# Value products of an attention group: two runs of five key tiles in place of four of two or three

## Chip, cores and metric

The kernel runs on one core of a Trainium2 chip. The metric is the device time in microseconds (us) from launch to end; three runs of the kernel before were timed. TensorE (PE in the rows; PEld is its loading of weights), VectorE (DVE), ScalarE (ACT) and GpSimd (POOL) each issue their instructions in one fixed order, and semaphores tie them together.

## What is computed

A trunk of two layers over 1024 latent and 256 context tokens. Each layer has an input projection, three head groups (latent attention, a convolution module, an mLSTM), an output projection with a norm, and an MLP with a norm. The change is in the latent attention. Cut to that part, the reference is:

```
def attend(q, k, v):
    s = einsum('bhqd,bhkd->bhqk', q, k) * 96 ** -0.5
    p = softmax(s, axis=-1)
    return einsum('bhqk,bhkd->bhqd', p, v)     # 8 heads, q and k of 96, v of 64 columns
```

There are 8 heads. Latent queries (1024) see 1280 keys, which are ten key tiles of 128; in the first layer the 256 context queries see the two key tiles of the context.

## The kernel before

`attention` (line 792) works on **groups** and **units**. A group is a pair of heads and 256 queries. A unit is one head and 128 queries, so a latent group has four units; they are called here the first, second, third and fourth unit of a group. The groups run over four head pairs, and within a pair over four latent blocks of 256 queries. In the first layer the fourth block of a pair has six units, since the two context units lie between its own.

For unit i the loop at line 987 issues, in this order:

- the **scores**: nine products in three chunks of keys (512, 512 and 256 columns), lines 77 to 79, tile `sc`. `sc` has 2560 columns, 1280 for the even units and 1280 for the odd ones; the two halves meet inside one bank of PSUM (columns 1024 to 1535);
- between the chunks, the **transposes** of the exponentials of unit i - 2 (line 936, ten blocks of 128 x 128 in parts of four, four and two), each part into one bank of PSUM (`et_ps`) and from there by ScalarE to the buffer `et` (line 84);
- the **softmax** (lines 908 to 911): VectorE reads the unit's scores from PSUM, negates them and takes the row minimum on the way (called the read below), ScalarE takes the exponentials and their sums, VectorE the reciprocals (`rb`);
- what `plan` holds for unit i. `at(i, ...)` appends to it. `values(G, j0, j1, fin)` (line 948) issues the value products of group G for the key tiles j0 to j1 (line 861, tile `pv`), for each tile one of either head: the two heads take the two halves of TensorE's columns. A product of f32 operands is two instructions, so a key tile is four. With `fin` it also issues `norm` (line 864): two transposes of the reciprocals on TensorE, two instructions on VectorE (lines 870 and 871), and `spill` (line 497): a copy and a subtraction on GpSimd and two stores from the SP queue. `qproj` (line 837) projects the queries of one head of the next group: six products on TensorE into a bank (`q_ps`), and its splitting on VectorE and ScalarE (`qf`, `kq`).

```
for k, (j0, j1) in enumerate(((0, 3), (3, 5), (5, 8), (8, 10))):
    at(f + 6 + k, lambda G=G, j0=j0, j1=j1: values(G, j0, j1, j1 == 10))
```

Here f is the number of the group's own first unit. A group of four units thus has its value products behind the scores of the next group's third unit (three key tiles) and fourth unit (two), and of the first unit (three) and second unit (two, and `norm`) of the group after that. The projections for the next group stand behind the second and third unit. While the convolution's taps last, one tap of it on VectorE (line 443) follows the scores of three units in four.

`et_ps`, `q_ps` and some other tiles share two banks of PSUM (pool `aux`, line 1997, `bufs=2`). A bank comes free when ScalarE or VectorE has read what is in it.

The order that each engine gets is set when the kernel is built: a planner of the framework takes instructions in the order in which the program issues them, but where by its own account of durations the next one of an engine would wait, it puts a later one that is ready ahead of it. On the chip each engine then keeps that order.

Of the kernel before, what the change touches and what calls it, by code (L numbers as in the profile page):

```python
# [33 lines left out]
# columns of the regrouped input projection: a0 g0 | a1 g1 | mq | mk | mv mg | mo | cq ckv kr  # L34
COL_CONV, COL_MQ, COL_MK, COL_MV, COL_MO, COL_CQ = 0, 512, 768, 1024, 1296, 1552

# per-partition constants of a layer
# [8 lines left out]
class Kern:  # L46
# [11 lines left out]
    # ---------------------------------------------------------------- helpers  # L58
# [4 lines left out]
    def after(self, ins, prev):  # L63
        """issue ins behind prev (same engine)"""
        self.tc.add_manual_dep(ins.ins, prev.ins.name, mybir.DependencyInfo(
            mybir.DependencyClass.NoSync, mybir.DependencyReason.DATA), reason="pace")
        return ins

    def release_held(self, prev, n=1):
        """the n oldest sets of transposes kept back are issued behind prev"""  # L70
        for _ in range(min(n, len(self.held))):
            for ins in self.held.pop(0):
                self.after(ins, prev)
# [20 lines left out]
    def rsqrt_steps(self, pool, out, x, scale, eps, n):  # L94
        """out = 1 / sqrt(x * scale + eps) on [p, n], from an integer estimate and Newton steps; an instruction a step."""
        p = out.shape[0]
# [14 lines left out]
    def rsqrt_act_steps(self, pool, out, x, scale, eps, n=1):  # L111
        """The same from ScalarE's square root and a Newton step."""
# [18 lines left out]
    # ---------------------------------------------------------------- set-up  # L131
# [28 lines left out]
    def ada_steps(self, l, rounds, raw_pool, ps, sm_pool, bufs, sm_tag="ada_bs", tag="wada", ahead=None, div=1):  # L160
        """Modulation vectors, four 512-column chunks a round: 0 sh1 sc1, 1 g1 sh2, 2 sc2 g2. A list of closures,
        each the products of one loaded piece and the load of a later one."""
# [48 lines left out]
    def ada_first(self, raw_pool, ps, sm_pool, bufs):  # L211
        """sh1 and sc1 of the first layer by halves of the features. A closure a half."""
# [3 lines left out]
        def half(h):  # L216
# [4 lines left out]
            # even k in the rows 0:64, odd k in the rows 64:128  # L221
# [20 lines left out]
    # ---------------------------------------------------------------- split streams: hi / lo tiles [128, tile, k, 128 tokens]  # L242
# [14 lines left out]
    def make_u0(self, u, tmp, kk):  # L257
        """The modulated stream of the first layer, four feature blocks."""
# [9 lines left out]
    # ---------------------------------------------------------------- input projection  # L268
    def load_w(self, pool, src, c0, n, tag="w"):
        """columns c0:c0+n of a [128, 8, N] weight as split tiles of four k each."""  # L270
# [25 lines left out]
    # ---------------------------------------------------------------- phase 1: everything read from the modulated stream  # L296
    def p1_mlstm(self, l, u, last, ps, wp, hk, ml, steps, w=None):
        """mLSTM query (feature-major), key, value and gates (token-major)."""
# [12 lines left out]
        # the first layer's stream comes by halves of its features  # L311
# [36 lines left out]
    def residual_steps(self, l, pool):  # L348
        """Closures: alpha * (normalised stream * ln2_g + ln2_b) of the layer before, a token tile each, in place."""
# [16 lines left out]
    def residual_consts(self, l, pool, tag, bufs):  # L366
        """Constant part of the second residual, alpha * ln1_b + g2 * b_mlp2, of both kinds of tokens to DRAM."""
# [10 lines left out]
    def p1_conv(self, l, u, last, ps, wp, tmp):  # L378
        """Gated linear unit of the conv group (twice its value; the halves are in the taps)."""
# [17 lines left out]
    def p1_mla(self, l, u, last, ps, wp, wx, raw):  # L397
        """Compressed q / kv and the rotary key of a token tile, with the mean squares of their rms norms."""
# [25 lines left out]
    # ---------------------------------------------------------------- conv: depthwise taps, layer norm over channels, swish  # L424
    def conv_steps(self, l, last, ps, acc, tp, pool):
        """Closures in order: taps of channel half 0 on VectorE, half 1 on GpSimd, then the norm and swish."""
# [7 lines left out]
        def tap(t, dve, pool_):  # L434
            # behind the given instructions of the two engines
# [61 lines left out]
    def spill(self, pool, c, t0, src):  # L497
        """256 tokens of a row block of the concatenated heads, split and kept in DRAM until the output projection."""
# [6 lines left out]
    # ---------------------------------------------------------------- bidirectional mLSTM  # L505
    def mlstm_gates(self, ps, gp, sm):
        """Stabilised gate quantities. Row r = dir * 64 + tile * 4 + head, tokens along the free axis."""
# [70 lines left out]
        # decay of every chunk on the partitions of its head  # L578
# [15 lines left out]
    def mlstm(self, l, last, ps, ml, wk):  # L594
        nc = self.nc
        nto = NLT if last else NT
        # chunk states: every chunk's own update goes to its successor's slot, then the recurrence runs in place
# [72 lines left out]
    def mlstm_out(self, l, u, last, pm, wp, S, wk):  # L670
        """Output gate from its own projection, per-head normalisation of a pair of token tiles; its rows of the
        concatenated heads."""
# [18 lines left out]
        def pair(t0):  # L691
# [6 lines left out]
            # statistics of the eight (tile, head) rows; H holds twice the gated value  # L698
# [12 lines left out]
    # ---------------------------------------------------------------- latent attention  # L711
    def mla_norm(self, l, last, gi, tmp):
        """Normalised compressed q / kv of a group of tokens, in place."""
# [11 lines left out]
    def mla_rotate(self, tmp):  # L725
        """Rotary shared key, in place."""
# [13 lines left out]
    def mla_prep(self, l, last, ps, A, tmp, gi):  # L740
        """Compressed q / kv and the shared key of a group of tokens, feature-major, the former split."""
# [28 lines left out]
    def mla_values(self, l, ps, wq, A):  # L770
        """Values of all heads, token-major."""
# [20 lines left out]
    def attention(self, l, last, psc, ps, X, wq, A1, A, B, wqk0, taps, post):  # L792
        """Software pipeline over units of (head, 128 queries): scores of unit i are issued between the transposes of
        unit i - 2, the value products of an earlier group and the projections of a later one. The units of the
        context queries (256 of a head in one) lie between those of the last latent group of their head pair."""
        nc, a = self.nc, self.a
        sc = psc.tile([P, 2560], F32, name="sc")
        # buffers in the place of the stream: transposed exponentials; split keys and queries
# [116 lines left out]
        def transpose_parts(i, E, kts):  # L915
# [11 lines left out]
            while i0 < nk:  # L927
                # runs of consecutive key tiles, four to a bank
# [25 lines left out]
        for G, (p, g) in enumerate(groups):  # L954
# [6 lines left out]
            if g < 3 or last:  # L961
                units += [(G, *x) for x in four]
                tap_at |= {f, f + 1, f + 2}
                for k, (j0, j1) in enumerate(((0, 3), (3, 5), (5, 8), (8, 10))):
                    at(f + 6 + k, lambda G=G, j0=j0, j1=j1: values(G, j0, j1, j1 == 10))
# [53 lines left out]
    # ---------------------------------------------------------------- rows, norms  # L1019
# [5 lines left out]
    def row_stats(self, pool, r, sm, tagp, junk, jb=2):  # L1025
        """(-mean, 1/std, -mean/std) of a token tile [128, 1024]; its row sums are in sm, else VectorE alone takes them."""
# [15 lines left out]
    def row_stats_steps(self, pool, st, r, sm, junk, jb, root=False):  # L1042
        """The same from row sums, the instructions behind the squares one by one."""
# [12 lines left out]
    def norm_rows(self, pool, r, sm, tagp, junk, jb=2):  # L1056
        """r = (r - mean) * rstd over the 1024 columns of a token tile."""
        st = self.row_stats(pool, r, sm, tagp, junk, jb)
        return self.nc.scalar.activation(r, r, AF.Identity, scale=st[:, 1:2], bias=st[:, 2:3])

    def next_stream(self, ps, x, t0, nt, rows, sc, sh, tmp, tag, hold=False):
        """rows: normalised token tiles t0..t0+nt; writes x = split(rows^T * sc + sh)."""
# [13 lines left out]
    def affine_cols(self, l, g0, b0, sc, sh, name):  # L1076
        """per-feature scale and shift of a modulated layer-normed stream: g*sc1, b*sc1 + sh  ([128, k, 2])"""
# [9 lines left out]
    # ---------------------------------------------------------------- output projection, first layer norm  # L1087
# [3 lines left out]
    def to_mats(self, ps, rows, sc, sh, pool, hold=False):  # L1091
        """rows: an even and an odd normalised token tile. For each kk the blocks B of rows^T * sc + sh (feature blocks
# [1179 lines left out]
```

## Time and profile before

| what | us |
|---|---|
| three runs of the kernel | 3289.71, 3295.98, 3297.98 |
| median of the runs | 3295.98 |
| span of the profiled execution, first to last instruction | 3292.5 |
| attention of the first layer, in the span | about 386 to 746 |
| attention of the second layer, in the span | about 2136 to 2469 |

The profiled execution shows its span and no time beside it; the span lies inside the three runs, 3.5 us under their median. In the rows a line is: start in us from the span's start, duration in us, engine, line of the kernel, operation, tile written and tiles read, shapes, how many were merged into the row (x12), and in brackets the idle time before it with what ended it. Matmuls are pipelined: one that shows 0.39 us may have its successor start 0.23 us after it, so distances between starts tell more than durations.

### The profile page before, as it was taken

The page shows a single profiled execution, that of the slowest core. Times are in us where ns is not written, and L with a number is a line of the kernel's source. Part 1 is how long each engine was busy: PE and PEld are TensorE (multiplying, and loading weights), DVE is VectorE, ACT ScalarE, POOL GpSimd, SP SyncE. Part 2 cuts the span into 40 slices and gives each one's busy share as a digit, 9 for nine tenths or more (in the row PEclk, how much of TensorE's full clock was granted, in tenths as well). Part 3 has the DMA queues.
Part 4 walks back from the last instruction along what each step waited for, and adds up shares of the span by engine and source line. Part 5 has one row for each costly group of instructions (what it writes and reads, how often), then busy time and mean ns, then how long its engine had stood idle before and what let it go on. Part 6 is the DMA issues. An engine that isn't in the chain of part 4 may idle for free.

```text
span 3292.5 us, 49295 instructions
## 1 busy us (share of the span) xinstructions
PE 3124.8 (95%) x18778; PEld 2540.8 (77%) x18778; DVE 2153.8 (65%) x3914; ACT 1356.8 (41%) x2572; POOL 1322.3 (40%) x1138
## 2 busy tenths in 40 slices
PE   7999999999899999999998999999999899999986
PEld 4778877777789999766677777877767799977775
DVE  3275688755854433767779445588757855578997
ACT  2122566672433333432332621466663433343332
POOL 0021488320221111466665251266411422258885
PEclk9999999999899999999999998999999899999998
DMA  8521100026433233444334332100025333333322
GB/s 263 187 68 40 49 18 17 14 83 225 159 120 101 97 99 103 157 126 144 114 109 134 142 111 50 56 21 14 14 92 213 109 109 108 106 128 97 102 94 105
DMA packets 179021, 337.17 MB, mean 102 GB/s; under 512 B 14016, under 2 KB 85696, under 8 KB 178784
## 3 DMA queue, kind: packets, MB, share of 16 engines
q1 hardware_dynamic: 178784, 334.03, 31.6%
q8 instruction: 147, 2.41, 0.3%
q14 instruction: 90, 0.74, 0.1%
HBM read 253.05 MB, written 80.92 MB: 101 GB/s over the span
## 4 chain that ended last, share of the span: by engine, by line
PE 71%; DVE 14%; issue 5%; POOL 3%; ACT 3%; DMA 3%; SPq 0%; DVEq 0%; POOLq 0%; ACTq 0%
PE c_ps L1365 18%; PE o_ps L1365 13%; PE pv L861 4%; PE et_ps L936 4%; PE ada L185 3%; PE cx_ps L1365 3%; DVE acc L2168 2%; PE sc L77 2%; PE sc L78 2%; PE sc L79 2%; PE o_ps L658 1%; PE y_ps L79 1%; DMA W<-md 1%; POOL h_s L2168 1%; PE y_ps L77 1%
## 5 line engine op out<-in xcount | busy, mean ns | idle before, releaser
L1365 PE MATMUL c_ps<-xs_hi,wm 128*128 128x256 f32 x2560 | 511.1, 288 | 11.5 <-DVE rw L2168 8.1
L1365 PEld LDWEIGHTS c_ps<-xs_hi,wm 128*128 128x128 f32 x2560 | 422.1, 195 | 38.7 <-DVE hb L1427 11.7
L1365 PE MATMUL o_ps<-xs_hi,xs_lo 128*128 128x512 f32 x1458 | 380.1, 398 | 27.8 <-DVE acc L2168 20.7
L1365 PE MATMUL c_ps<-xs_lo,wm 128*128 128x256 f32 x1280 | 366.6, 286 | 3.2 <-DVE xs_lo L2168 3.2
L1365 PEld LDWEIGHTS o_ps<-xs_hi,xs_lo 128*128 128x128 f32 x1458 | 271.9, 190 | 120.8 <-DVE acc L2168 34.6
L2168 DVE TENSOR_TENSOR acc<-o_ps,acc 128x512 f32<-128x512 f32 x405 | 271.8, 683 | 101.7 <-PE o_ps L1365 99.4
L1365 PEld LDWEIGHTS c_ps<-xs_lo,wm 128*128 128x128 f32 x1280 | 249.6, 195 | 3.9 <-DVE xs_lo L2168 3.6
L84 ACT COPY et<-et_ps 128x512 f32<-128x512 f32 (+1 forms) x392 | 198.4, 515 | 97.7 <-PE et_ps L936 93.1
L1365 PE MATMUL c_ps<-bx,wm 128*128 128x256 f32 x1536 | 229.2, 288 | 4.5 <-ACT bx L2168 3.0
L92 DVE TENSOR_TENSOR wm<-rw,wm 128x512 fp32r<-128x512 f32 x175 | 140.2, 803 | 111.2 <-ACT wm L84 110.4
L1365 PE MATMUL o_ps<-wm,xs_lo 128*128 128x512 f32 x783 | 208.0, 397 | 4.4 <-DVE acc L2168 3.5
L1365 PEld LDWEIGHTS c_ps<-bx,wm 128*128 128x128 f32 x1536 | 205.2, 195 | 7.9 <-ACT bx L2168 3.5
L84 ACT CAST wm<-rw 128x512 fp32r<-128x512 f32 x175 | 108.4, 620 | 231.2 <-PE c_ps L1365 177.8
L1395 POOL TENSOR_TENSOR w_s<-w_s,rw 128x512 f32<-128x512 f32 x30 | 40.0, 1332 | 397.3 <-DVE wm L92 397.3
L861 PE MATMUL pv<-et,V 128*64 128x256 f32 x1312 | 193.3, 391 | 0.0
L1365 PEld LDWEIGHTS o_ps<-wm,xs_lo 128*128 128x128 f32 x783 | 147.5, 191 | 50.8 <-DVE acc L2168 8.6
L77 PE MATMUL sc<-kq 128*128 128x512 f32 (+1 forms) x400 | 165.9, 415 | 8.4 <-DVE E L908 7.4
L1429 ACT ACTIVATE hb<-c_ps,fm 128x256 f32<-128x256 f32 x240 | 112.8, 474 | 144.3 <-PE c_ps L1365 137.6
L2168 POOL TENSOR_TENSOR xs_hi<-rw,xs_hi 128x512 fp32r<-128x512 f32 x94 | 138.4, 1487 | 78.9 <-ACT xs_hi L2168 78.8
L449 POOL TENSOR_TENSOR conv_acc<-conv_acc,tap 128x656 f32<-128x656 f32 x120 | 154.5, 1287 | 8.8
L908 DVE TENSOR_SCALAR_CACHE_REDUCE E<-sc 128x1280 f32<-128x1280 f32 x91 | 135.2, 1486 | 26.7 <-PE sc L79 25.9
L909 ACT ACTIVATE E<-E,nm 128x1280 f32<-128x1280 f32 x91 | 124.4, 1368 | 66.4 <-DVE E L908 66.1
(506 smaller groups left out, 7968.6 us busy)
## 6 DMA issues: line engine op xcount, KB each, us to landing
rw<-in_w_mlp SPq DMA_DIRECT2D x126, 512.0 KB
hb<-h_d SPq DMA_DIRECT2D x72, 512.0 KB
h_d<-hb SPq DMA_DIRECT2D x64, 512.0 KB
wada<-in_w_ada SPq DMA_DIRECT2D x48, 512.0 KB
wada<-in_w_ada SPq DMA_DIRECT2D x96, 256.0 KB
cat_d<-sp SPq DMA_DIRECT2D x144, 128.0 KB
w_raw<-in_w_in SPq DMA_DIRECT2D x20, 512.0 KB
xs_hi<-cat_d SPq DMA_DIRECT2D x18, 512.0 KB
```

The lines of the kernel that those rows point to most:

```text
L77: mm(ps, lh, rh, start=first, stop=False)
L79: return mm(ps, ll, rh, start=False, stop=last)
L84: return nc.scalar.copy(out, in_)
L92: return h, e.tensor_tensor(lo, src, hi.bitcast(F32), ALU.subtract)
L449: nc.gpsimd.tensor_tensor(aj[:, c], aj[:, c], m, ALU.add)
L861: nc.tensor.matmul(pvs[G][64 * e:64 * e + 64, 0], self.V[:, kt, h * 64:h * 64 + 64], ets[G, e][:, kt], start=(i == 0), stop=(i == nk - 1))
L908: dve = nc.vector.tensor_scalar(E, s[:, c], -1.0, None, ALU.mult, ALU.min, accum_out=nm[:, 0:1])
L909: act = nc.scalar.activation(E, E, AF.Exp, bias=nm[:, 0:1], scale=-1.0, accum_out=nm[:, 1:2])
L936: nc.tensor.transpose(pt[:, j], E[:, (i0 + j) * P:(i0 + j + 1) * P], self.ident)
L1365: ins = self.nc.tensor.matmul(ps, x, y, start=first and i == 0, stop=i == len(todo) - 1, skip_group_check=True)
L1429: self.nc.scalar.activation(h[:, :, q], b, AF.Identity, bias=f[:, FM_B1 + 2 * i + q % 2:FM_B1 + 2 * i + q % 2 + 1])
L2168: ins = f(*a, **k)
```

## The change

The four entries of a group in `plan` become two: key tiles 0 to 4 behind the scores of unit f + 6, key tiles 5 to 9 and `norm` behind those of unit f + 8. Nothing stands in `plan` for the group at f + 7 and f + 9 any more. The number of value products, their operands and their order are the same. The groups of six units in the first layer keep their own entries. The other parts of the diff only empty comments and docstrings; line numbers stay the same.

```diff
             if g < 3 or last:
                 units += [(G, *x) for x in four]
                 tap_at |= {f, f + 1, f + 2}
-                for k, (j0, j1) in enumerate(((0, 3), (3, 5), (5, 8), (8, 10))):
-                    at(f + 6 + k, lambda G=G, j0=j0, j1=j1: values(G, j0, j1, j1 == 10))
+                for k, (j0, j1) in ((6, (0, 5)), (8, (5, 10))):
+                    at(f + k, lambda G=G, j0=j0, j1=j1: values(G, j0, j1, j1 == 10))
             else:
```

## Rows read from the trace of the kernel before

**Rows 1.** Windows, both attentions: length, busy PE PEld DVE ACT POOL, PE clock, DMA, GB/s.
```profile
386.00:746.00 360.00, 354.39 (x2316) 258.53 (x2315) 278.77 (x554) 234.43 (x449) 201.33 (x185) 1.00 0.13 39
2136.00:2469.00 333.00, 325.60 (x2145) 238.98 (x2143) 246.57 (x457) 216.74 (x396) 159.60 (x173) 1.00 0.12 36
```

**Rows 2.** Timeline of TensorE over four units, third to second, second layer.
```profile
2342.44 0.39 PE L77 MATMUL sc<-kq 128*128 128x512 f32 x1
...
2344.94 0.29 PE L79 MATMUL sc<-kq 128*128 128x256 f32 x1
...
2345.38 1.51 PE L861 MATMUL pv<-et,V 128*64 128x256 f32 x12
2346.83 0.39 PE L77 MATMUL q_ps<-cqn,wqk_s 128*128 128x256 f32 x1
...
2347.67 0.50 PE L77 MATMUL sc<-kq 128*128 128x512 f32 x1
...
2350.07 0.28 PE L79 MATMUL sc<-kq 128*128 128x256 f32 x1
2350.19 0.60 PE L936 MATMUL et_ps<-ident,krT 128*128 128x128 f32 x4
2350.72 1.08 PE L861 MATMUL pv<-et,V 128*64 128x256 f32 x8
2351.73 0.55 PE L936 MATMUL et_ps<-ident,E 128*128 128x128 f32 x3
2352.03 0.48 PE L77 MATMUL sc<-kq 128*128 128x512 f32 x1
...
2354.30 0.29 PE L79 MATMUL sc<-kq 128*128 128x256 f32 x1
...
2354.73 1.52 PE L861 MATMUL pv<-et,V 128*64 128x256 f32 x12
...
2356.26 0.48 PE L77 MATMUL sc<-kq 128*128 128x512 f32 x1
...
2358.53 0.28 PE L79 MATMUL sc<-kq 128*128 128x256 f32 x1
...
2360.19 0.44 PE L868 MATMUL pv<-ident,rb 128*128 128x128 f32 x2
2360.38 0.36 PE L77 MATMUL q_ps<-cqn,wqk_s 128*128 128x256 f32 x1
...
2361.18 0.39 PE L77 MATMUL sc<-kq 128*128 128x512 f32 x1
```

**Rows 3.** Timeline of VectorE in the same stretch: two reads, a subtraction, the norm's copy.
```profile
2344.69 1.51 DVE L92 TENSOR_TENSOR kq<-qf,kq 128x256 fp32r<-128x256 f32 x1 [0.58 <-ACT kq L84]
2346.13 1.48 DVE L908 TENSOR_SCALAR_CACHE_REDUCE E<-sc 128x1280 f32<-128x1280 f32 x1
...
2350.39 1.49 DVE L908 TENSOR_SCALAR_CACHE_REDUCE E<-sc 128x1280 f32<-128x1280 f32 x1 [0.46 <-PE sc L79]
...
2360.73 0.42 DVE L870 COPY rsb<-pv 128x256 f32<-128x256 f32 x1 [0.39 <-PE pv L868]
```

**Rows 4.** Waits of TensorE for VectorE's read, one stage each (us in total, times, longest).
```profile
PE sc L77 <- DVE E L908: 2.1, 6, 0.5
...
PE sc L77 <- DVE E L908: 3.4, 4, 1.3
```

**Rows 5.** Waits of weight loads, first layer's attention: entries into value runs.
```profile
PEld pv L861 <- issue: 12.3, 72, 0.4
```

**Rows 6.** Timeline of ScalarE: copies out of the two banks behind the fourth unit.
```profile
2350.03 0.59 ACT L84 COPY et<-et_ps 128x512 f32<-128x512 f32 x1 [0.29 <-PE et_ps L936]
2350.82 0.59 ACT L84 COPY et<-et_ps 128x512 f32<-128x512 f32 x1 [0.21 <-PE et_ps L936]
```

**Rows 7.** Timeline of TensorE at a run of value products that the planner has cut.
```profile
449.61 0.65 PE L861 MATMUL pv<-et,V 128*64 128x256 f32 x2
450.19 0.44 PE L936 MATMUL et_ps<-ident,E 128*128 128x128 f32 x2
```

## Prediction

> **What bounds the kernel now.** I first read the windows over the two attention stages, since the change touches nothing else [rows 1]. TensorE shows 354.39 us busy in 360 and 325.60 in 333, VectorE 278.77 and 246.57, at a granted clock of 1.00. By that, TensorE would be full, and whatever leaves its queue would be gained. A page of the Trainium skill, Perfetto Trace Analysis (Identifying the Most-Contended Engine), says that the busy share of matmuls is a poor measure, because they are pipelined, and points to weight loading; that reads 258.53 of 360 here. Read by the busy share the change would be worth the whole price of the runs it removes; read by starts, as I do below, most of that is given back.
>
> So I went on to the timeline of TensorE over four regular units [rows 2] and of VectorE beside it [rows 3]. What is to be seen is a chain from unit to unit. The scores of the fourth unit end with the product at 2350.07. VectorE's read of them starts at 2350.39 and takes 1.49. The next scores start at 2352.03, behind it. Behind the third unit it is the same, and tighter: the read ends at 2346.13 + 1.48 = 2347.61, and the scores start at 2347.67. No score product of these four units starts before the read of the unit before has ended, though `sc` has two halves; and where TensorE waits at the start of scores, it is this read that it waits for [rows 4]. So a unit is a **score phase** and then a **window**, from the start of its last score product to the first of the next unit. The window cannot be shorter than 0.32 + 1.49 + 0.06 = 1.87 us. What TensorE has to do in it is free up to that length; what is missing in it is a wait.
>
> The four score phases [rows 2] take 2.50 (third unit), 2.40 (fourth), 2.27 (first) and 2.27 (second), the windows 2.73, 1.96, 1.96 and 2.65: together 18.74 us for a group. The two windows without a projection, behind the fourth and the first unit, are 1.96 against a floor of 1.87: the value products fill them almost exactly. That is what the four runs do.
>
> **The change part by part.** I count by group. Twelve groups of the first layer and sixteen of the second have the four runs. The last group of the second layer comes when no scores are left, so 27 groups matter.
>
> *Runs removed.* A run of two key tiles takes from 2350.72 to 2351.73, 1.01 us, one of three from 2354.73 to 2356.18, 1.45 [rows 2]. A key tile is 0.44, and 0.13 remains for leaving. Entering: a transpose takes 0.10 to 0.11 (three at 2351.73 take 0.30), so the last of the four at 2350.19 starts at about 2350.52; the run begins 0.20 later, where another transpose would follow after 0.11, so 0.09. A run costs 0.22 beside its products; its entry also shows as a wait of the weight loads, 72 times in the first stage, 12.3 us or 0.17 each [rows 5]. Two runs fewer: 0.44 us a group, 12 us over 27, if TensorE were bound by its own work alone.
>
> *Windows after.* A run of five takes 1.01 + 3 x 0.44 = 2.33. Behind the first unit: 0.43 from the last score product to the run (2354.30 to 2354.73), 2.33, and the norm's pair, 0.19 (2360.19 to 2360.38): 2.95. Behind the third: 0.43 + 2.33 + 0.84 for the projection (2346.83 to 2347.67): 3.60. Behind the second: four transposes end 0.55 after the last score product (0.11 + 4 x 0.11), the projection takes 0.80 (2360.38 to 2361.18), 1.35, so the floor, 1.87, with 0.52 idle. Behind the fourth: 0.55, so again 1.87, with 1.32 idle. The sum is 10.29 against 9.30: **0.99 us more**.
>
> *Score phases after.* They shrink where the planner moves transposes of the coming unit into an idle window, as it does with three at 2351.73 [rows 2]; each is worth 0.11. With none moved, the phases are like the third and fourth of before, 2 x (2.50 + 2.40) = 9.80, 0.36 more than the 9.44 of now. Into 0.52 idle go four, into 1.32 eight, if banks are free. At the fourth unit one bank is free when the copy ends at 2350.62 and the other when the next one ends at 2351.41 [rows 6]; four transposes can start at once and four more fit before 2351.94, just so. With four and eight moved the phases are 9.80 - 1.31 = 8.49, and the group is 0.99 - 0.95 = **+0.04**. With four and four it is +0.48, with none +1.35. Downwards, the planner can also move a value product or two into what is left idle; the bound is the full 0.44 gained. I take +0.20 a group: between eight and four moved, nearer to eight because it fills such gaps wherever something is ready [rows 2, 7]. Over 27 groups that is +5.4 us.
>
> *Late reads.* VectorE's reads are sometimes late: the one at 2346.13 stands behind a subtraction of 1.51 us and starts 0.90 after its scores (2344.94 + 0.29) end [rows 2, 3]. The windows behind the first and third unit grow by about 1 us each and cover such lateness. The waits that could go are part of 2.1 and 3.4 us [rows 4]; I count -2 us, since those behind the second and fourth unit stay.
>
> *Norm.* It moves one unit earlier, with two TensorE transposes (counted), two VectorE instructions of 0.42 [rows 3], its GpSimd pair and two stores. The first unit's longer window covers VectorE's two; were that cover gone, they would make the next read late by 0.84 at most. On GpSimd they stand ahead of a tap instead of behind it, and nothing waits for that; the stores are read only by the output projection. Order and number in SP's queue stay. Buffers: the transposed exponentials are read at f + 8 at the latest, a unit earlier than now, so no new wait.
>
> **Sum.** 5.4 - 2 = +3.4 us on the profiled execution's span of 3292.5: 3295.9. The median of the runs stands 3.5 above that span, so I give **3299** as the time that a median would show. About 0.3%, or 9.9 us, is what a measurement of this kernel can tell from no change, so this is the same.
>
> **The rivals.**
>
> *Faster: everything idle is filled.* The planner cuts the next run and puts pieces of it into the windows behind the second and fourth unit, as it did at 449.61, two value products ahead of two transposes [rows 7]. The cost of the cut then falls into idle time. TensorE stays dense and the runs' price comes home: 27 x 0.44 = 12, with the 2 us of late reads 14, so 3282. For it: idle of 1.32 is long enough for eight transposes and a key tile. Against it: a piece of two, as there, is one head alone and takes 0.58 to the next start where both heads would take 0.57. The Trainium skill, TensorEngine Tiling (Array Packing), Key Properties, says that a change of tiling mode drains TensorE; by that alone fewer runs are faster, and the trace agrees that a run has a price, but not that TensorE is all that binds. Chance 0.24.
>
> *Slower: the bank.* The projection behind the second unit is no longer behind a value run, so its six products take one of the two banks about 1.2 us sooner, and hold it until VectorE comes to read it. Through the window and into the third unit's scores the transposes then have one bank, and each part waits for ScalarE's copy of 0.59 [rows 6]. The four moved there fall away, 0.44, and with four at the fourth unit the group is 0.48 + 0.44 = +0.92: 25 us, less the 2, so 3319. It decides from +0.44 a group on, where 27 x 0.44 less 2 is 9.9. For it: VectorE is busy for three quarters of the stage [rows 1]. Against it: the planner keeps account of the banks and can take other work first. Chance 0.28.
>
> *It does not do what it says.* The planner cuts the runs so that there are again about four a group. Then prices and covers are as now: 3296, inside "the same", 0.15 of its 0.48.
>
> **How the numbers follow.** Same 0.48 (the forecast and the last rival; its own range is 3287 to 3306), faster 0.24, slower 0.28. The range of 8 in 10 is 3281 to 3316: down to the dense case, 3282, and well into the slower one, which begins at 3306. Left out are the upper end of that one (3319, and 3332 with nothing moved), some 0.13, and some 0.05 below.
>
> **What would show it.** Right: a group of four units near 18.9 us; windows of about 1.9 behind the second and fourth unit and 2.9 and 3.6 behind the other two; score phases of the first and third unit near 2.0; six to eight transposes just ahead of the first unit's scores; fewer entries than 72; more waits of scores for VectorE's read behind the fourth unit. Wrong: windows of the second and fourth unit full of value products and a group of 18.4 (the faster rival), or a group over 19.1 with transposes waiting for copies in the third unit's scores (the slower one).

## Result and the profile after

The changed kernel is slower. The first comparison, five runs of each, gave 3315.83 us against 3297.98: a ratio of 1.0066, with a 95% interval of 1.0047 to 1.0084. A second one, with 12 runs of the changed kernel and 35 of the one before (the first experiment below), gave 3305.62 against 3292.86: 1.0036, 1.0016 to 1.0056. The forecast was no change, 3299.

**Where the time is.** The first profiled execution has a span of 3314.0, 21.5 more than before. I cut it at the first and the last score product of each attention stage; from here on a stage is that stretch, and the windows below are set on it. The columns are start and end, length, and the busy time of PE, PEld, DVE, ACT and POOL, then PE clock, DMA share and GB/s. The kernel before:

```profile
376.62:731.82 355.20, 349.63 (x2259) 256.94 (x2258) 278.00 (x547) 234.79 (x445) 202.35 (x185) 0.99 0.10 30
2128.67:2452.25 323.58, 316.56 (x2071) 234.58 (x2069) 244.87 (x460) 216.35 (x395) 161.39 (x175) 1.00 0.09 25
```

The changed kernel, which answers to [rows 1]:

```profile
387.14:750.19 363.05, 354.71 (x2267) 261.10 (x2267) 277.76 (x549) 235.19 (x446) 200.33 (x185) 1.00 0.10 29
2141.57:2470.08 328.51, 326.63 (x2077) 241.81 (x2077) 234.85 (x457) 217.92 (x395) 157.20 (x175) 1.00 0.09 26
```

The stages grew by 7.9 and 4.9. Length less busy time is TensorE's idle time, and that is the main reading: it went from 5.6 to 8.3 in the first stage and fell from 7.0 to 1.9 in the second, while busy time rose by 5.1 and 10.1. The change was to take work off TensorE, and by these rows it put 15 us on it.

Another 10.5 us lie ahead of the attention: its first score product comes at 387.14, not 376.62, although the order of the instructions on every engine is the same up to there. The granted clock differs. Between 250 and 300 us, before and after:

```profile
250.00:300.00 50.00, 49.25 (x308) 41.20 (x308) 27.31 (x60) 7.76 (x11) 4.70 (x4) 0.97 0.14 40
```

```profile
250.00:300.00 50.00, 49.25 (x217) 38.12 (x218) 23.55 (x54) 4.39 (x6) 3.86 (x2) 0.73 0.01 2
```

TensorE is busy for 49.25 of 50 in both, but at a mean clock of 0.73, that is, for more than half of the stretch at 1.2 GHz in place of 2.4, it gets through 217 matmuls where it did 308. Over the whole stretch ahead of the attention, the same 2111 matmuls took 376.62 us at a mean clock of 0.97 before and 387.14 at 0.94 after; in other executions of this study they took 370.75 at 0.98 and 390.67 at 0.92. What made the clock fall in one execution and not in another is open. The rest of the span, behind the stages and between them, makes up the difference with -1.8.

**Four units after.** The timeline of TensorE in the second layer, fourth to third unit, answers to [rows 2]:

```profile
2342.31 0.40 PE L77 MATMUL sc<-kq 128*128 128x512 f32 x1
...
2344.59 0.28 PE L79 MATMUL sc<-kq 128*128 128x256 f32 x1
2344.71 0.60 PE L936 MATMUL et_ps<-ident,E 128*128 128x128 f32 x4
2345.20 0.66 PE L936 MATMUL et_ps<-ident,krT 128*128 128x128 f32 x4
2345.78 0.65 PE L861 MATMUL pv<-et,V 128*64 128x256 f32 x2
2346.36 0.55 PE L936 MATMUL et_ps<-ident,krT 128*128 128x128 f32 x3
2346.66 0.48 PE L77 MATMUL sc<-kq 128*128 128x512 f32 x1
...
2348.48 0.28 PE L79 MATMUL sc<-kq 128*128 128x256 f32 x1
...
2348.91 2.37 PE L861 MATMUL pv<-et,V 128*64 128x256 f32 x18
2351.21 0.44 PE L868 MATMUL pv<-ident,rb 128*128 128x128 f32 x2
2351.41 0.48 PE L77 MATMUL sc<-kq 128*128 128x512 f32 x1
...
2353.77 0.28 PE L79 MATMUL sc<-kq 128*128 128x256 f32 x1
...
2355.64 0.50 PE L77 MATMUL sc<-kq 128*128 128x512 f32 x1
...
2357.80 0.29 PE L79 MATMUL sc<-kq 128*128 128x256 f32 x1
2358.02 0.65 PE L861 MATMUL pv<-et,V 128*64 128x256 f32 x2
2358.60 0.44 PE L936 MATMUL et_ps<-ident,E 128*128 128x128 f32 x2
2358.97 2.37 PE L861 MATMUL pv<-et,V 128*64 128x256 f32 x18
2361.27 0.39 PE L77 MATMUL q_ps<-cqn,wqk_s 128*128 128x256 f32 x1
...
2362.09 0.40 PE L77 MATMUL sc<-kq 128*128 128x512 f32 x1
```

A product has two records, so a key tile of both heads is x4 and a run of five tiles is x20. There is no x20: each run is cut into x2, one head's product of one tile, and x18. The windows are 2.07 (fourth unit), 2.93 (first), 1.87 (second) and 4.29 (third), the phases 2.28, 1.82, 2.36 and 2.16: 19.78 for the group, against 18.74 in the rows of before.

That 18.74 was a short group. Measured from third unit to third unit, the second layer's groups take 18.4 to 24.9 before (18.73 for the one in the rows, 19.2 for three others) and 19.2 to 24.8 after, where seven of fifteen are at 19.8. That is the regular group of what follows, taken in the same way from every kernel. The group of the rows grew by 1.05, two of the three in which a new pair of heads begins shrank by 2.4 and 2.5, and all fifteen together grew by 4.4.

Over the whole trace the entries into value runs went from 170 to 157, and those of a single product rose from 39 to 70; 37 runs are x18. The first layer's own count, of [rows 5], says as much (72 before):

```profile
PEld pv L861 <- issue: 11.0, 60, 0.4
```

### The profile page after: what moved, and what is told of

Its sections match the earlier page's. It is cut to its first block, busy times and chain, and to the rows that moved or that the text cites. A ratio compares the mean times of both kernels' runs of the same rounds, so it can differ in the third digit from the quotient of the medians.

```text
span 3314.0 us, 49278 instructions
## 1 busy us (share of the span) xinstructions
PE 3146.4 (95%) x18778; PEld 2559.2 (77%) x18778; DVE 2144.9 (65%) x3914; ACT 1357.9 (41%) x2572; POOL 1315.9 (40%) x1138
## 3 DMA queue, kind: packets, MB, share of 16 engines
q8 instruction: 147, 2.41, 0.3%
## 4 chain that ended last, share of the span: by engine, by line
PE 70%; DVE 14%; POOL 4%; issue 4%; DMA 4%; ACT 3%; SPq 0%; DVEq 0%; POOLq 0%; ACTq 0%
PE c_ps L1365 18%; PE o_ps L1365 12%; PE pv L861 5%; PE et_ps L936 4%; PE ada L185 3%; PE cx_ps L1365 3%; DVE acc L2168 3%; PE sc L77 2%; PE sc L78 2%; PE sc L79 2%; PE o_ps L658 1%; DMA W<-md 1%; PE y_ps L79 1%; DVE rw L2168 1%; DVE xs_lo L2168 1%
## 5 line engine op out<-in xcount | busy, mean ns | idle before, releaser
L861 PE MATMUL pv<-et,V 128*64 128x256 f32 x1312 | 202.3, 388 | 0.4 <-DVE rsb L871 0.4
L908 DVE TENSOR_SCALAR_CACHE_REDUCE E<-sc 128x1280 f32<-128x1280 f32 x91 | 135.4, 1488 | 38.1 <-PE sc L79 37.6
L936 PE MATMUL et_ps<-ident,E 128*128 128x128 f32 x910 | 148.4, 278 | 4.1 <-ACT et L84 2.4
```

The lines of the kernel that those rows point to most:

```text
L861: nc.tensor.matmul(pvs[G][64 * e:64 * e + 64, 0], self.V[:, kt, h * 64:h * 64 + 64], ets[G, e][:, kt], start=(i == 0), stop=(i == nk - 1))
L908: dve = nc.vector.tensor_scalar(E, s[:, c], -1.0, None, ALU.mult, ALU.min, accum_out=nm[:, 0:1])
L936: nc.tensor.transpose(pt[:, j], E[:, (i0 + j) * P:(i0 + j + 1) * P], self.ident)
```

## Experiments

"Whole" stands for this edit, in every kernel whose name has it and in those said to have whole runs: the first product of a run is ordered behind the last transposes of its own unit, so that the scheduler can hardly take one ahead (7 entries of a single product are left, of 70).

```
 def pvmm(G, i, first=False):
...
+                if first and e == 0 and tlast:
+                    self.after(ins, tlast[-1])
```

The edit moves line numbers: in these kernels the transposes are at L938 or L941 (L936 before), VectorE's read at L910 or L913 (L908 before).

The two stages of every kernel, from first to last score product, with TensorE's idle time (length less busy) in brackets, and the ratio to the kernel before with its interval. The stages are from one profiled execution each; a kernel without a ratio ran once.

| kernel | first stage | second stage | ratio |
|---|---|---|---|
| before | 355.2 (5.6) | 323.6 (7.0) | |
| changed, again | 362.8 (8.3) | 328.5 (1.9) | 1.0036, 1.0016 to 1.0056 |
| changed, whole | 361.4 (17.9) | 323.8 (10.6) | 1.0015, 0.9995 to 1.0036 |
| whole, projection behind fourth unit | 368.4 (20.8) | 319.1 (9.3) | 1.0030, 1.0013 to 1.0047 |
| whole, runs behind fourth and first | 362.3 (22.7) | 330.3 (18.0) | 1.0034, 1.0015 to 1.0054 |
| before, whole | 353.4 (12.9) | 328.4 (13.4) | 1.0003, 0.9987 to 1.0020 |
| before, no taps between | 338.0 (1.6) | 308.4 (2.6) | |
| changed, whole, no taps between | 342.5 (8.4) | 315.9 (9.3) | |
| whole, heads apart | 395.0 (13.1) | 360.9 (10.0) | |
| whole, four runs at the context units | 360.0 (18.2) | 324.0 (10.5) | |
| whole, projection first | 355.1 (14.5) | 327.0 (11.1) | 1.0001, 0.9987 to 1.0016 |
| before, whole, projection first | 354.3 (15.0) | 321.2 (7.2) | 1.0003, 0.9981 to 1.0025 |
| mixed | 353.1 (12.9) | 319.2 (8.1) | 0.9983, 0.9969 to 0.9998 |

### The changed kernel again

No edit.

> The changed kernel once more, nothing edited. In the first profiled execution the first score product of the first attention stage came 10.5 us later than before (387.14 against 376.62) although no engine's instruction order differs up to there, and the granted clock showed 0.73 from 250 to 300 us where before it showed 0.97. Theory 'chance': that part is a property of the execution, so here the first score product comes anywhere from 374 to 390, while the regular group of the second layer is again 19.78 within 0.05 and the two attention stages together, first to last score product, are again 10 to 15 us longer than before. Theory 'systematic': 387 again, within 1 us, at the same clock.

The first score product came at 370.75, at this clock between 250 and 300 us:

```profile
250.00:300.00 50.00, 49.25 (x332) 42.56 (x331) 29.08 (x71) 8.84 (x15) 2.21 (x3) 1.00 0.16 47
```

The stages were again 12.5 us longer (7.6 and 4.9), the regular group 19.79. So the late start did not come again, and "systematic" is out; "chance" holds, though its range of 374 to 390 was too narrow: over all kernels of this study the first score product lies between 370.8 and 390.7, a spread of 20 us that is no part of the change. The stages repeat within 0.3 us, so what follows is read from them. Their 12.5, less some 1 us in the stretches behind them (133.96 and 113.45 to the last product of the output projection's first part, before 137.59 and 110.89), agree with the 0.36% of the second comparison.

### Whole runs

> The changed kernel, with the first value product of each run ordered behind the last transposes of its own unit, so that the scheduler cannot take single products ahead: entries into value runs fall from 157 to 77, those of a single product from 70 to 7. Theory 'cuts' (the loss is the price of runs cut into one head's product and nine others: each cut costs one key tile more, 0.43, and one entry and exit more, together about 0.66, two in a group): the regular group falls from 19.78 to 18.6 to 18.9, the windows to about 2.9, 1.9, 3.5 and 1.9, and the time to 3285 to 3300, level with before. Theory 'covers' (the loss is the two windows that lost their runs, and transposes that wait for a bank there): the group stays at 19.4 or above with TensorE waiting for VectorE's reads and ScalarE's copies, and the time is 3310 or more.

The regular group was 18.92 (0.02 above the range of "cuts"), its windows 2.82 (first unit), 1.87, 3.65 and 2.01; the time 3297.93. A run of five tiles and the next start, in the timeline of TensorE:

```profile
2362.82 2.38 PE L861 MATMUL pv<-et,V 128*64 128x256 f32 x20
2365.13 0.38 PE L77 MATMUL q_ps<-cqn,wqk_s 128*128 128x256 f32 x1
```

It takes 2.31 from start to start. Above, x18 took 2358.97 to 2361.27, 2.30: nine products cost what ten do, and the tenth, cut off, took 2358.02 to 2358.60, 0.58, besides. With 0.09 for its entry a cut costs 0.67, and the 37 at the runs of x18 cost 25 us. TensorE's busy time fell by about that (columns as above):

```profile
390.67:752.09 361.42, 343.56 (x2267) 258.78 (x2267) 278.47 (x550) 235.20 (x446) 199.63 (x185) 0.99 0.10 29
2147.93:2471.78 323.85, 313.30 (x2078) 238.42 (x2077) 235.22 (x459) 216.70 (x395) 160.51 (x175) 1.00 0.09 26
```

11.1 and 13.3 us less than in the first profile after, 24 in sum. The near agreement with 25 is no proof, since more than 37 cuts went: entries fell by 80. An estimate over all pieces, with 0.24 for each (0.09 to enter, 0.15 to leave) and 0.43 for each tile or lone product, has the value products' own time fall by 19 and 22 us, more than the busy time did.

In the second stage "cuts" holds: 323.8 is the length before. That is a net effect, since 8.7 us of the 13.3 came back as idle time. In the first it does not hold: 9.5 of the 11 us came back. The waits of TensorE in the first stage name the largest part (us in total, times, longest):

```profile
PE et_ps L938 <- DVE qf L846: 5.5, 7, 1.1
PE sc L77 <- DVE krT L910: 3.7, 5, 1.0
```

The first is a transpose that waits for VectorE to take a projection out of its bank; in the changed kernel it is 0.9 us:

```profile
PE et_ps L936 <- DVE qf L846: 0.9, 3, 0.5
```

### The projection behind the fourth unit

Whole runs, and:

```
-                at(f - 2, lambda G=G: qproj(G, 1))
+                at(f - 1, lambda G=G: qproj(G, 1))
```

> As the run with whole five-tile runs, and besides the projection of the second head goes from behind the third unit to behind the fourth, so that runs (third and first unit) and projections (second and fourth) alternate. Theory 'cuts': windows of about 2.8, 1.9, 2.9 and 1.9, the group 18.2 to 18.5 and the time 3275 to 3290, faster than before by the price of the two runs removed (0.24 each, 27 groups, 13 us). Theory 'covers': TensorE waits in the windows of the second and the fourth unit, the group is 18.9 or above and the time 3300 or more.

The windows came as expected (2.84, 1.87, 3.03 and 1.87), and the second stage is 4.5 us shorter than before; but the regular group is 18.72, not 18.2 to 18.5, since the phases sum to 9.1: few transposes are moved out of them now. The first stage is 13 us longer than before, with 15 more idle; 5.7 us of it are transposes that wait for VectorE to read a projection, six times. The time, 3306.31, missed the 3275 to 3290 of "cuts".

### Runs behind the fourth and first unit

Whole runs, and:

```
-                for k, (j0, j1) in ((6, (0, 5)), (8, (5, 10))):
+                for k, (j0, j1) in ((7, (0, 5)), (8, (5, 10))):
```

> Two whole runs of five tiles, but behind the fourth unit and the first of the next group, which have no projections, in place of behind the third and the first. Theory 'cuts': windows of about 3.0 (fourth), 2.9 (first), 1.9 and 1.9, the group 18.4 to 18.8, the time 3280 to 3297. Theory 'covers': the windows behind the second and third unit wait as in the run with whole runs alone, 19.2 or above and 3305 or more.

The group was 19.50 and the time 3306.51: a miss for "cuts". The windows were 2.96 (fourth unit), 2.93 (first), 1.87 (second) and 2.41 (third). The third unit's has lost its cover, and VectorE's late read shows in it:

```profile
2352.75 0.50 PE L77 MATMUL sc<-kq 128*128 128x512 f32 x1 [0.56 <-DVE E L910]
```

That is the theory "covers", at this place; the second unit's window does not wait. The phases take 9.3 of the group, 0.7 more than in the run with whole runs alone, so the window is not all of the loss.

### The kernel before with its runs whole

> The kernel before, with its four runs of two or three tiles kept whole in the same way (the first product of each ordered behind the last transposes of its own unit): entries fall from 170 to 124, those of a single product from 39 to 4. Counted by entries, 0.68 for each and 0.43 for each further tile, the own time of the value products falls by 24 us. Theory 'cuts cost here too': the attention stages become 5 to 15 us shorter in sum and the time is 3278 to 3289 on a level of before of 3293. Rival 'they fill waits': the single products stand where TensorE would wait for VectorE anyway, in the first layer above all; the stages change by less than 3 us and waits for VectorE grow from 2.1 us to 8 or more in the first layer.

The first stage gained 1.9 us, the second lost 4.8: "fill waits" has it for the sum, but not for the place. It expected the waits for VectorE's reads to grow to 8 us in the first layer, where they went from 2.5 to 3.8 only. Idle time grew by 7.3 and 6.4. In the second stage TensorE waits for VectorE's reads, as in [rows 4], but more (in this stage it was 4.9 and 0.4 before):

```profile
PE sc L77 <- DVE E L910: 7.8, 6, 3.2
PE sc L77 <- DVE krT L910: 2.2, 4, 1.7
```

So in this kernel the order edge that keeps runs whole is not free, and a single product taken ahead seems no loss where TensorE would have waited; which product filled which wait was not followed.

### Heads apart

Whole runs, and the five products of one head ahead of those of the other:

```
-            for j in range(j0, j1):
-                pvmm(G, j, j == j0)
+            for e in range(2):
+                for j in range(j0, j1):
+                    pvmm(G, j, j == j0, (e,))
```

> The changed kernel with whole runs, but each run's five products of one head first and then the five of the other. Theory 'a head alone takes as long as both' (only products of the two heads side by side overlap): a run of ten takes 4.3 us in place of 2.3, the regular group of the second layer grows from 18.9 to about 23.2 and the time by 100 to 125 us. Rival 'only ends cost' (the price of a cut is the entry and the exit alone): the run stays at 2.3 to 2.7 and the group under 19.8.

```profile
2208.57 3.72 PE L861 MATMUL pv<-et,V 128*64 128x256 f32 x20
2212.23 0.39 PE L77 MATMUL q_ps<-cqn,wqk 128*128 128x256 f32 x1
```

The run takes 3.66 and the group 21.6: between the two expectations. The time of the one execution, 3383.0, is 85 us above that of the run with whole runs, where "a head alone" expected 100 to 125. Inside the run the records of a lone head start 0.216 apart, so a product takes 0.43, as long as the pair's; where the heads meet, four records of the second start beside the first's last ones, which saves some 0.8. Most of the overlap that the pair has is lost. The Trainium skill, TensorEngine Tiling (Array Packing), Key Properties, says that different tiles can execute matmuls in parallel, and that a change of tiling mode drains the engine. The trace agrees on the first: the pair's records start 7 ns apart. A run costs about 0.24 beside its products, which fits the second, though no row names a drain. The rows add that half of the array alone is no faster.

### Without taps between the units

Two kernels, the one before and the changed one with whole runs:

```
-                    if i in tap_at:
+                    if False:
...
+        while taps:
+            taps.pop(0)(pace[-1][:2])
```

> The kernel before with all 31 conv taps and the norm behind them issued after the last unit of each attention stage and not between its units (the work is the same, the total grows by it). It is the base for the next run. Both theories: the attention stages shorten by the late reads of VectorE, 2 to 15 us in the first layer; TensorE's waits for VectorE there stay under 2.1 us.

> The changed kernel with whole runs, its taps issued behind the attention stages in the same way. With taps its first layer was 6.1 us longer than before, and there TensorE's transposes waited 5.5 us, in 7 places, for VectorE to take a projection out of a bank. Theory 'the bank' (VectorE, late with taps and slow copies, holds the projection's bank): without taps these waits fall under 1 us and the first layer is at most 2.5 us longer than that of the kernel before without taps. Rival 'pile-up' (the run, the projection and the keys of the groups with context queries come into one window): the difference stays at 4.5 us or more.

The totals, 3672.6 and 3680.2, hold the taps behind the stages. The base is 17.2 us shorter in the first stage, a little more than expected:

```profile
383.32:721.28 337.96, 336.33 (x2218) 250.98 (x2218) 195.92 (x463) 224.87 (x420) 30.29 (x47) 1.00 0.07 20
```

With whole runs:

```profile
373.39:715.92 342.53, 334.15 (x2228) 254.66 (x2227) 192.90 (x465) 225.44 (x421) 26.55 (x44) 0.99 0.07 20
```

The waits there, longest first, begin with

```profile
PE et_ps L938 <- ACT et L84: 3.7, 10, 0.7
```

and hold none for a projection, as "the bank" has it; but the difference to the base is still 4.6 us, as the rival has it, and 7.5 in the second stage. With VectorE relieved, the kernel before leaves TensorE 1.6 us idle. Two long runs save 2.2 us of busy time in the first stage and leave 6.7 more idle: by the sum, the windows that lost their runs are not filled. Each of the two kernels ran once.

### Four runs at the context units

Whole runs, and:

```
+                for k, (j0, j1) in ((6, (0, 3)), (7, (3, 5)), (8, (5, 8)), (9, (8, 10))) if not last and g == 2 else ((6, (0, 5)), (8, (5, 10))):
```

> The changed kernel with whole runs, but in the first layer the four runs of before for the group whose products fall among the units with context queries (the third of each head pair). Without taps whole runs were still 4.6 us longer than before in that layer, 1.3 us in each of the four groups with context units. Theory 'pile-up' (there a run of ten, a projection and the next pair's keys come into one window, 4.94 us long, while the short context unit's window has nothing): those four groups lose 1 us or more each and the first layer, first to last score product, comes to 357.5 or less from 361.4. Rival 'moved' (the work that leaves them goes into the next pair's first group, which was 0.7 to 3 us shorter than before): the first layer stays at 360 or more.

The first stage came to 360.0 in one execution, so "moved" holds, just; by this the groups with context units are not the place.

### The projection ahead of the run

Whole runs; both projections stand ahead of the value products of their unit, and a run is ordered behind them too:

```
-                at(f - 2, lambda G=G: qproj(G, 1))
+                plan.setdefault(f - 2, []).insert(0, lambda G=G: qproj(G, 1))
```

> The changed kernel with whole runs, and the second head's projection ahead of the run of ten in the third unit's window and not behind it, so that VectorE has the length of the run to take it out of its bank. With whole runs alone the first layer was 8.1 us longer than with four whole runs (361.4 against 353.4), and its transposes waited 5.5 us for VectorE's read of a projection. Theory 'the bank': these waits fall under 1 us and the first layer comes to 357 or less; the second stays at 323.8 within 2 us. Rival 'the windows' (the two windows left without a run cost it, wherever the projection is): the waits go, but other waits take their place, and the first layer stays at 359.5 or more.

> The control: the kernel before with its four runs whole and the projections ahead of the runs. With four runs the transposes waited only 0.8 us for a projection's bank in the first layer, so theory 'the bank' expects at most 1.5 us from it there (353.4 to between 351.5 and 354). In the second layer, where four whole runs came to 328.4 with waits for VectorE's reads in the groups with key projections, nothing is expected of it: 326 to 330. The rival expects the same.

First what this is about. In the run with whole runs alone, TensorE and VectorE behind a third unit:

```profile
519.46 0.40 PE L79 MATMUL sc<-kq 128*128 128x512 f32 x1
520.91 0.66 PE L938 MATMUL et_ps<-ident,krT 128*128 128x128 f32 x4 [1.05 <-DVE qf L846]
```

```profile
519.12 0.16 DVE L912 RECIPROCAL nm<-nm 128x1 f32<-128x1 f32 x1 [1.58 <-ACT E L911]
519.32 1.20 DVE L87 COPY rb<-nm 128x64 f32<-128x64 f32 x1
520.45 0.41 DVE L846 TENSOR_TENSOR qf<-q_ps,ropeT 128x256 f32<-128x256 f32 x1
```

The projection ended ahead of the fourth unit's scores; its read stands behind a copy that takes 1.20 here, and the transposes inside those scores wait for the bank. With the projection ahead of the run:

```profile
504.36 0.39 PE L77 MATMUL q_ps<-cqn,wqk_s 128*128 128x256 f32 x1
...
505.25 2.38 PE L863 MATMUL pv<-et,V 128*64 128x256 f32 x20
507.55 0.50 PE L77 MATMUL sc<-kq 128*128 128x512 f32 x1
...
509.28 0.60 PE L941 MATMUL et_ps<-ident,krT 128*128 128x128 f32 x4
```

The wait is gone from the whole stage, which comes to 355.1, level with before: "the bank" holds. The second stage missed, 327.0 in place of 323.8. Its regular group takes 19.2 in place of 18.92, with a third window of 3.86 for 3.65, and in the last group of three head pairs that window takes 5.4 for 4.3; why is open. In the control the first stage is 354.3, 0.3 beyond the bound; its second stage missed as well, 321.2 where 326 to 330 was expected.

### Mixed

Four whole runs in the first layer; in the second two whole runs, with the second head's projection behind the fourth unit.

> The first layer as in the run with four whole runs, the second as in the run with two whole runs and the second head's projection behind the fourth unit. If the stages simply add: first layer 352.7 to 353.5 (before 355.2), second 319 (before 323.6), together 6 us less than before, a ratio of 0.998, which 5 rounds may just show. Rival: a stage's gain is given back behind it, in the output projection; then the stages are as said and the stretch from the last score product to the end of the output projection's first part (137.6 and 110.9 us before) is longer by 3 us or more.

```profile
373.87:726.93 353.06, 340.19 (x2259) 254.19 (x2258) 278.12 (x547) 235.54 (x445) 201.48 (x185) 1.00 0.10 30
2122.37:2441.59 319.22, 311.12 (x2078) 238.30 (x2077) 229.63 (x459) 216.35 (x395) 161.21 (x175) 1.00 0.09 26
```

The stages simply add, 6.5 us less than before, and behind them little is given back (136.2 and 113.2, where it was 137.6 and 110.9). With 0.9983 this version is faster than the kernel before, by little, and so than the changed one.

## Why the prediction was wrong

**The floor of a window**: right. 1.87 behind the second unit is what the account of scores, read and scores gave.

**Windows and phases for whole runs**: right for the group that was counted. With whole runs it is 18.92 where 18.74 + 0.20 was forecast; behind the fourth unit nine transposes were moved, of which eight were forecast, and the window is 0.14 longer than the floor.

**The step that failed**: the sum counts a run of five as whole, 2.33, and its term for the two runs removed is -0.44 a group, 12 us. The third rival did foresee that the planner might cut the runs again into four a group, as it did at [rows 7], but says of it that "prices and covers are as now". That took the price of a cut to be that of an entry, 0.22. The prediction has the fact that speaks against this, that a piece of one head takes 0.58 where both heads would take 0.57; it uses it against the faster rival and not here: the other head's product then takes as long again by itself. A cut between the heads costs 0.67, three times the run price.

What the runs showed in its place: the entries into value runs went from 170 to 157 and not down by two for each of 27 groups, and more of them are single products. By the estimate over all pieces (0.24 each, 0.43 for a tile or a lone product) the value products' own time in the two stages grew by 3.0 and 8.8 us. Of the two cuts in a regular group only one is paid in full: against whole runs the third window is 4.29 for 3.65, but the fourth is 2.07 for 2.01, since there the piece stands where transposes would (seven are moved into that window, not nine). Of the 0.86 that the group lost to the cuts, 0.64 is the third window.

**27 equal groups**: wrong, in two ways. The four units that were counted are a short group of the kernel before: their window behind the fourth unit is 1.96, filled "almost exactly", but in nine of the fifteen groups it is 2.1 to 4.6. And the group was taken from the second layer and multiplied. In the second stage removing the cuts gives 4.7 of the 4.9 back; in the first it gives 1.4 of 7.6, since there VectorE then holds a bank, a wait that the sum has at nothing. With that mended too, the stage is at its old length. The projection ahead of runs that are not whole was not tried, so how the 7.6 divide between the two is open.

Had the runs stayed whole, as the sum has it, the stages would have grown by 6.2 and 0.3 where +3.4 was forecast in all, and the time would show no clear change (1.0015, 0.9995 to 1.0036). That the total is near is in part luck: the sum has the same gain or loss in every group, and nearly all of the loss is in the first stage.

**Late reads, -2**: the direction is right. In the second stage the waits of scores for VectorE's reads fell from 5.3 to 0.4, before and after:

```profile
PE sc L77 <- DVE E L908: 4.9, 5, 1.4
```

```profile
PE sc L77 <- DVE E L908: 0.4, 1, 0.4
```

In the first stage they grew from 2.5 to 3.3. Together that is 4.1 less.

**The rivals.** "Everything idle is filled" came true in the second stage, 1.9 us idle in 328.5, and it was slower all the same: what filled the gaps was the cuts' price. "The bank" gave 3319, near the first comparison's 3315.8, but that nearness is luck: in the changed kernel its mechanism is 0.9 us of waits. With whole runs it is 5.5 us, and it is the third unit's projection, behind a run, that VectorE fetches late; I had it at the second unit's. (The 3332 given for its upper end leaves out the 2 us of late reads: 27 x 1.35 less 2 on 3296 is 3330.)

**The runs' price**, 0.22 a run, was about right: entry and leaving are 0.24. Whether two runs fewer save the 12 us is not shown. With whole runs busy time is 6.1 and 3.3 us less than in the kernel before, but that kernel has cuts too. Against the kernel before with its runs whole, busy time is 3.1 more in the first stage and 1.7 less in the second.

**Open**: in the first stage, whole runs without taps stay 4.6 us longer than the base, with 6.7 more idle. Transposes waiting for ScalarE's copies are 3.7 of that, waits of scores for VectorE's reads 1.4; the rest is in gaps too short for the rows to name what ended them. Why the projection ahead of the run costs the second stage 3.2 us is open too.

## What to carry to other kernels

A list in program order is not the order that runs. Where a scheduler fills gaps, ask at which instruction it will cut, and what the rest of a pair costs alone; then pin what must stay together, but only where no wait is there to be filled. When two stages run the same loop beside different work, cost the change in each; and check that the one you count is like the others. Compare stages between fixed instructions, for here the start alone scattered by 20 us, more than the change is worth.

## What the runs showed of the hardware

- A value product of one head on half of the array takes 0.43, as long as both heads' side by side: from its start to that of the next instruction a piece of one product takes 0.58 and one of two 0.58, nine products take 2.30 and ten 2.31.
- A copy of 128x64 on VectorE takes 0.2 us in the median of the first stage and up to 1.35 beside taps, which run on GpSimd too; without the taps its longest was 0.88. In the kernel before, all 26 copies there that took over 0.4 ran beside a GpSimd instruction, and the 28 with none beside them took under 0.2. That GpSimd is the cause is only argued: 15 others ran beside one and were as short.
- With an unchanged order of instructions the clock granted between 250 and 300 us was 0.97, 0.73 and 1.00 in three executions, with TensorE busy for 49.25 of 50 in each. Up to the attention the same 2111 matmuls took 370.75 us at a mean clock of 0.98 and 390.67 at 0.92.
